# Output projection and SwiGLU by seven block products, tokens stationary, with two of four weight sums made by accumulating DMAs

## The chip, the cores and the metric

One core of a Trainium2 chip runs the whole program. The metric is the device time in microseconds (us) of one execution, as the median of several runs.

## What is computed

One encoder block over 512 tokens of 2048 features, everything in float32. Cut to what matters here:

```python
h = rms_norm(x, norm_mix)
z = h @ w_in                                   # q, k, v, u and two gates
merged = gate_a * (y_a @ w_branch_a) + gate_b * (y_b @ w_branch_b)
x = x + merged @ w_out                         # 2048 x 2048: the output projection
gu = rms_norm(x, norm_ffn) @ w_gate_up         # 2048 x 11264
x = x + (silu(gu[..., :5632]) * gu[..., 5632:]) @ w_down     # 5632 x 2048
return rms_norm(x, norm_final)
```

`y_a` is chunked attention and `y_b` a pooling mixer; the change leaves both as they are.

## The kernel before, in words

Activations lie with features on the partitions and the 512 tokens along the free axis. A float32 operand is split exactly into two float32r parts, `hi` and `lo = value - hi`, and each product is three matmuls into one PSUM group: lo x hi, hi x hi, hi x lo. In `product` (L183 to L186) the weights are the stationary operand (128x128) and the tokens move (128x512).

Weights come in units of four contraction tiles by 256 output columns (512 KB). For each unit SP issues one load (L123), ScalarE (ACT) makes `hi` (L132), VectorE (DVE) makes `lo` (L141). A unit's 24 matmuls follow in `panel` (L188), which then runs `step()`: one step of each side job in the list `active` (evacuations, norms, splits of activations), and then the `lo` of a unit three ahead. Each engine works through its own instructions in the order in which the code emits them, and so do the two DMA queues used, SP's and GpSimd's (POOL's).

The stages in order: q, k, v with attention beside them; u and the pooling mixer; gates and merge, where `evac_a` (L669) leaves a merged tile in `T` and `merged` (L674) splits it into `MH`, `ML`; the output projection (`evac_o`, L712, adds the residual, which comes back from `xt_dram`); SwiGLU in four blocks of hidden tiles, gate and up panels (`evac_g`, `evac_up`) and then the down panels, which add into `X1` in `evac_d` (L804). The last four hidden tiles are multiplied with tokens stationary (L859 to L863), so that the last sums, the final norm and the stores go token tile by token tile (`evac_y`, `store`).

## Time and profile before

| | us |
|---|---|
| median of 3 runs (2622.86 to 2624.26) | 2624.05 |
| span of the profiled execution, first to last instruction | 2621.3 |
| PE (TensorE) busy in it | 2608.7 |
| DVE busy | 1040.0 |
| ACT busy | 757.8 |

The profile gives only the span of its execution, not a time of its own; the median of the runs lies 2.75 us above it, which is taken as what lies around a span. A matmul's row lasts 0.39 us, since matmuls are pipelined; the distance between two starts is its cost. Idle time of DVE, ACT and POOL costs nothing by itself; PE's does.

### The profile page before, as it was taken

Reading aid. Unit: us, or ns where it says so; the run is one execution under the profiler, and the core shown is the slowest. Engines: PE = TensorE matmul, PEld = TensorE weight load, DVE = VectorE, ACT = ScalarE, POOL = GpSimd, SP = SyncE. Lnnn points to the kernel's source line nnn. Section 1 sums busy time; section 2 is a strip of 40 time slices with the busy share of each in tenths; the row PEclk is TensorE's granted clock in tenths of the full one; section 3 lists DMA queues with packets and bytes.
Section 4 is the critical chain, followed back from the end, with each engine's and each line's share of the span. In section 5 each row is a group of like instructions: output and inputs, shape, how many; then the busy total and the mean of one; then the engine's idle time right before and its main releaser. Section 6 shows DMA issues by size and latency. Waiting matters only on the chain.

```text
span 2621.3 us, 28748 instructions
## 1 busy us (share of the span) xinstructions
PE 2608.7 (100%) x11947; PEld 2158.0 (82%) x11947; DVE 1040.0 (40%) x1462; ACT 757.8 (29%) x1046; POOL 27.9 (1%) x75
## 2 busy tenths in 40 slices
PE   9999999999999999999999999999999999999998
PEld 7888888888888888888888888888888888888887
DVE  6455556433343334444333332333332333333353
ACT  5344433322232223232222212222212222222243
POOL 0000000000000000000000000000000000000003
PEclk9999999999999999999999999999999999999999
DMA  6422232233333333333333323333333332333242
GB/s 206 129 85 85 84 90 86 87 94 96 96 97 97 97 97 110 121 122 98 97 97 97 97 97 97 97 97 97 98 99 97 98 98 78 96 117 97 83 143 81
DMA packets 253474, 264.09 MB, mean 101 GB/s; under 512 B 9160, under 2 KB 241424, under 8 KB 253344
## 3 DMA queue, kind: packets, MB, share of 16 engines
q1 hardware_dynamic: 252032, 260.22, 31.7%
q8 instruction: 93, 1.52, 0.2%
q10 hardware_dynamic: 1152, 1.97, 0.2%
q14 instruction: 37, 0.30, 0.0%
q0 software_dynamic: 160, 0.07, 0.0%
HBM read 253.79 MB, written 8.43 MB: 100 GB/s over the span
## 4 chain that ended last, share of the span: by engine, by line
PE 99%; DMA 1%; ACT 0%; DVE 0%; issue 0%; SPq 0%; ACTq 0%; DVEq 0%
PE psd L184 30%; PE psd L186 30%; PE psd L185 30%; PE psd L430 1%; PE psd L432 1%; PE psd L431 1%; PE psa L477 1%; PE psa L557 1%; PE psa L523 1%; PE psa L476 1%; PE psa L186 0%; PE psa L184 0%; PE psa L185 0%; DMA wl<-in_w_down 0%; PE psa L323 0%; PE psa L799 0%
## 5 line engine op out<-in xcount | busy, mean ns | idle before, releaser
L141 DVE TENSOR_TENSOR lo<-raw,hi 128x1024 fp32r<-128x1024 f32 (+3 forms) x473 | 551.8, 1169 | 1142.3 <-ACT hi L132 1142.0
L132 ACT ACTIVATE hi<-raw 128x1024 fp32r<-128x1024 f32 (+3 forms) x473 | 477.7, 1012 | 1316.5 <-PE psd L186 1022.2
L185 PE MATMUL psd<-h2h,hi 128*128 128x512 f32 x1408 | 547.7, 389 | 0.0
L184 PE MATMUL psd<-h2h,lo 128*128 128x512 f32 x1408 | 547.7, 389 | 0.0
L186 PE MATMUL psd<-h2l,hi 128*128 128x512 f32 x1408 | 547.7, 389 | 0.0
L184 PE MATMUL psd<-xh,lo 128*128 128x512 f32 x864 | 341.4, 395 | 0.0
L185 PE MATMUL psd<-xh,hi 128*128 128x512 f32 x864 | 336.6, 390 | 0.0
L186 PE MATMUL psd<-xl,hi 128*128 128x512 f32 x864 | 336.6, 390 | 0.0
L185 PEld LDWEIGHTS psd<-h2h,hi 128*128 128x128 f32 x1408 | 264.3, 188 | 54.9
L186 PEld LDWEIGHTS psd<-h2l,hi 128*128 128x128 f32 x1408 | 264.3, 188 | 54.9
L184 PEld LDWEIGHTS psd<-h2h,lo 128*128 128x128 f32 x1408 | 264.3, 188 | 54.9
L184 PE MATMUL psd<-hidh,lo 128*128 128x512 f32 x640 | 250.5, 391 | 1.0 <-DVE xt L805 1.0
L186 PE MATMUL psd<-hidl,hi 128*128 128x512 f32 x640 | 249.1, 389 | 0.0
L185 PE MATMUL psd<-hidh,hi 128*128 128x512 f32 x640 | 249.0, 389 | 0.0
L184 PEld LDWEIGHTS psd<-xh,lo 128*128 128x128 f32 x864 | 162.2, 188 | 36.4 <-issue 2.4
L186 PEld LDWEIGHTS psd<-xl,hi 128*128 128x128 f32 x864 | 162.2, 188 | 34.2
L185 PEld LDWEIGHTS psd<-xh,hi 128*128 128x128 f32 x864 | 162.3, 188 | 32.0
L184 PEld LDWEIGHTS psd<-hidh,lo 128*128 128x128 f32 x640 | 120.1, 188 | 26.6 <-DVE xt L805 1.9
L186 PEld LDWEIGHTS psd<-hidl,hi 128*128 128x128 f32 x640 | 120.1, 188 | 25.1
L185 PEld LDWEIGHTS psd<-hidh,hi 128*128 128x128 f32 x640 | 120.2, 188 | 24.5
L185 PE MATMUL psd<-mh,hi 128*128 128x512 f32 x256 | 99.6, 389 | 0.0
L184 PE MATMUL psd<-mh,lo 128*128 128x512 f32 x256 | 99.6, 389 | 0.0
(197 smaller groups left out, 2345.1 us busy)
## 6 DMA issues: line engine op xcount, KB each, us to landing
raw<-in_w_gate_up SPq DMA_DIRECT2D x176, 512.0 KB, 3.5
raw<-in_w_in SPq DMA_DIRECT2D x127, 512.0 KB, 3.8
raw<-in_w_down SPq DMA_DIRECT2D x56, 512.0 KB, 3.5
raw<-in_w_out SPq DMA_DIRECT2D x32, 512.0 KB, 3.5
raw<-in_w_branch_b SPq DMA_DIRECT2D x16, 512.0 KB, 3.4
raw<-in_w_branch_a SPq DMA_DIRECT2D x16, 512.0 KB, 3.4
raw<-in_w_down SPq DMA_DIRECT2D x16, 384.0 KB, 3.3
xt_dram<-xt SPq DMA_DIRECT2D x16, 256.0 KB, 4.8
```

What stands on the lines that cost most here:

```text
L132: nc.scalar.activation(hi_t[i][:, :nk], raw_t[i][:, :nk], AF.Copy)
L141: nc.vector.tensor_tensor(lo_t[i][:, :nk], raw_t[i][:, :nk], hi_t[i][:, :nk].bitcast(F32), op=ALU.subtract)
L184: mm(ps, wl, ah, start=start, stop=False)
L185: mm(ps, wh, ah, start=False, stop=False)
L186: mm(ps, wh, al, start=False, stop=stop)
L430: mm(o, XH[kk][:, tok], hi[:, k], start=first, stop=False, skip_group_check=True)
L431: mm(o, XH[kk][:, tok], lo[:, k], start=False, stop=False, skip_group_check=True)
L432: mm(o, XL[kk][:, tok], hi[:, k], start=False, stop=final, skip_group_check=True)
L476: mm(o, q[:, tok], k[:, :n], start=True, stop=False)
L477: mm(o, q[hi_half, tok], kl[hi_half, :n], start=False, stop=True)
L523: nc.tensor.transpose(tp[b][:, o:o + P], sc[sb][:, sc0 + kt * P:sc0 + (kt + 1) * P], ident)
L557: mm(o_ps[:, kt * P:], VS[i, kt][:, hh * 2 * DH:(hh + 1) * 2 * DH], part[b][:, c:c + n], start=done == 0, stop=done == n_mm - 1)
```

## The change

The early stages, to the merge, stay as they are, apart from where tiles lie: the pool `slots` shrinks from 64 to 31 tiles, x^T has a pool of its own, x^T is no longer spilled to DRAM, and a merged tile goes from `evac_a` to `m_dram` by a POOL DMA in place of being split.

From the output projection on, three matrix products are cut into jobs. A job takes eight contraction tiles and 1024 output columns for all 512 tokens and is a 2x2 by 2x2 block product: the tokens fall into two halves, the contraction tiles into even and odd ones, the columns into two times 512. In place of eight block products it makes seven (Strassen's scheme in Winograd's form), `P1 P5 P6 P3 P7 P2 P4`, each in two units of 12 matmuls (two token tiles, two contraction tiles, three matmuls). Tokens are now stationary and weights move, 128x512. There are 36 jobs of 14 units and, at the end, two of 7 (half the contraction): four for `w_out`, 22 for `w_gate_up` (11 with the first half of the contraction, 11 with the second), 12 for `w_down`.

- **Token side**, `build_forms`: for each product a sum of token quarters is split into `hi` and `lo`, on ACT and DVE, as a generator that goes one product a `step()`. 19 halves are built.
- **Weight side**: of each unit pair the quarters 11, 22 and 21 are loaded. The sum 11+12 (tile `t1`) is a plain SP load of 11 and, behind it, a POOL DMA of 12 that accumulates into the same tile; 22+12 (`t3`) likewise. The other two sums, `t1`+22 and 21+(`t1`+22), are made by DVE in `t_to` (L851, L855). `hi2_to` (ACT, L863) and `lo2_to` (DVE, L871) split what a unit needs. The `t1` tiles have three buffers, and a `t1` is read until the sum for P4; the other quarters have six.
- **Outputs**: products accumulate in PSUM where the scheme allows it; what has to be combined is copied out by ACT after P1, P5, P6 (L906, L911, L916) and by DVE after P3, P7, P2 (L918, L923, L929); after P4 by DVE (L933) where an earlier partial result is added, else by ACT. Partial results and residuals are added by accumulating POOL DMAs into the tile (L908, L913, L920) or, in the `w_down` jobs but the last two, from the tile into DRAM (L1070); others are stored to DRAM by POOL DMAs (`x1p`, `x1d`, `gp`).
- **Turning**: since tokens come out on the partitions, `x1_ready` and `hidden` transpose on PE (`turned`, L960): 240 transposes of 128x128. The 64 transposes of the old end (L799) go.
- Between the merge and the first job `drain()` emits all steps of the first forms before the first unit's `hi` and `lo`.

The core of the diff:

```diff
-N_SLOTS = 64
+N_SLOTS = 31
...
+PRODUCTS = ("P1", "P5", "P6", "P3", "P7", "P2", "P4")
+NP = len(PRODUCTS)
+NPAIR = 4
+N_RAW2 = 6
+N_C = 6
+LOAD_AHEAD = 7
+T_BY_DMA = True
...
-        nc.vector.tensor_tensor(T[m], T[m], s, op=ALU.add)
...
-    def merged(ms):
-        for m in ms:
-            MH[m], ML[m] = split(T.pop(m), "m")
-            yield
...
+        nc.vector.tensor_tensor(s, T.pop(m), s, op=ALU.add)
+        m_dram[m] = tc.dram_tile([P, 512], F32, name=f"m_dram{m}")
+        nc.gpsimd.dma_start(m_dram[m], s)
...
+    def build_forms(forms, h, half):
+        a11, a12 = half[:, :, 0, 0:256], half[:, :, 1, 0:256]
+        a21, a22 = half[:, :, 0, 256:512], half[:, :, 1, 256:512]
...
+        tt = nc.vector.tensor_tensor
+        plan = [("P1", a11, 1, None), ("P5", s, 1, lambda: tt(s, a22, a21, op=ALU.subtract)),
+                ("P6", s, -1, lambda: tt(s, s, a11, op=ALU.add)),
+                ("P3", s, 1, lambda: tt(s, s, a12, op=ALU.subtract)),
+                ("P7", s3, 1, lambda: tt(s3, a11, a21, op=ALU.subtract)), ("P2", a12, 1, None), ("P4", a22, 1, None)]
+        for p, src, sign, make in plan:
+            if make:
+                make()
+            hi, lo = forms[p][:, prs, 0], forms[p][:, prs, 1]
+            nc.scalar.activation(hi, src, AF.Copy, scale=float(sign))
+            yield
+            if sign > 0:
+                tt(lo, src, hi.bitcast(F32), op=ALU.subtract)
+            else:
+                nc.vector.scalar_tensor_tensor(lo, src, -1.0, hi.bitcast(F32), op0=ALU.mult, op1=ALU.subtract)
+    def build_merged(forms, kb):
+        hs = []
+        for h in range(2):
+            half = yield from new_half()
+            for j in range(4):
+                nc.sync.dma_start(half[:, j // 2, j % 2], m_dram[8 * kb + 4 * h + j])
+            hs.append(half)
+            yield
+        for h in range(2):
+            yield from build(forms, h, hs[h])
+    for i in range(n_blk):
+        panel(KD, XH, XL, lambda oc, ps, i=i: evac_gate(2 * i + oc, ps))
+        if i == n_blk - 1:
+            XH = XL = None
+            xtiles.close()
...
+            active.append(build_merged(fo, 0))
+            spacing[0] = 0
+        panel(KA, YAH, YAL, lambda oc, ps, i=i: evac_a(2 * i + oc, ps))
+    drain()
+    midpool.close()
+    early.close()
...
+    class Job:
+        def quarter(self, s, f, h):
+            r0 = (self.k0 + 4 * h) * P
+            v = self.w[r0:r0 + 4 * P, self.c[f]:self.c[f] + 512]
+            return v.rearrange("(k s p) c -> s p k c", s=2, p=P)[s]
...
+    def plan_loads():
+        for j in jobs:
+            for h in range(j.nh):
+                loads.append((j.at("P1", h), j, "11", h))
+                loads.append((j.at("P5", h) - (4 if T_BY_DMA else 0), j, "t1" if T_BY_DMA else "12", h))
+                loads.append((j.at("P6", h), j, "22", h))
+                if T_BY_DMA:
+                    loads.append((j.at("P7", h) - 4, j, "t3", h))
+                loads.append((j.at("P2", h), j, "21", h))
...
+    def load2_to(n):
+        while loads and loads[0][0] <= n:
+            _, j, q, h = loads.pop(0)
+            t = rawtile(j, q, h)
+            s, f = {"11": (0, 0), "12": (0, 1), "21": (1, 0), "22": (1, 1), "t1": (0, 0), "t3": (1, 1)}[q]
+            nc.sync.dma_start(wide(t), j.quarter(s, f, h))
+            if q[0] == "t":
+                nc.gpsimd.dma_start(wide(t), j.quarter(0, 1, h), accum_op=ALU.add)
...
+        while st2["t"] < min(n, len(wunits)):
+            i = st2["t"]
+            j, p, h = wunits[i]
+            r = {q: t for (q, hh), t in j.raw.items() if hh == h}
+            run = r.get("t1", r.get("11"))
+            lo2_to(i - j.nh + 1)
...
+            elif p == "P6":
+                nc.vector.tensor_tensor(run, run, r["22"], op=ALU.add)
...
+            elif p == "P4":
+                nc.vector.tensor_tensor(r["21"], r["21"], run, op=ALU.add)
+            st2["t"] += 1
+    def hi2_to(n):
+        while st2["hi"] < min(n, len(wunits)):
+            i = st2["hi"]
+            t_to(i + 1)
+            hi_t[-1 - i] = staged("hi", f"w{i}")
+            nc.scalar.activation(hi_t[-1 - i], source(i), AF.Copy)
+    def lo2_to(n):
+        while st2["lo"] < min(n, len(wunits)):
+            i = st2["lo"]
+            hi2_to(i + 1)
+            lo_t[-1 - i] = staged("lo", f"w{i}")
+            nc.vector.tensor_tensor(lo_t[-1 - i], source(i), hi_t[-1 - i].bitcast(F32), op=ALU.subtract)
...
+        X = Y = Z = None
+        a = p5 = u2 = None
+        for n, p in enumerate(PRODUCTS):
...
+            for h in range(j.nh):
+                i = j.base + n * j.nh + h
+                load2_to(i + LOAD_AHEAD)
+                t_to(i + SPLIT + 1)
+                hi2_to(i + SPLIT)
+                hi, lo = wide(hi_t.pop(-1 - i)), wide(lo_t.pop(-1 - i))
+                for t in range(2):
+                    for k in range(2):
+                        fh, fl = forms[p][:, 2 * h + k, 0, TOK[t]], forms[p][:, 2 * h + k, 1, TOK[t]]
+                        last = h == j.nh - 1 and k == 1
+                        mm(ps[:, t], fh, lo[:, k], start=first, stop=False, skip_group_check=True)
+                        mm(ps[:, t], fh, hi[:, k], start=False, stop=False, skip_group_check=True)
+                        mm(ps[:, t], fl, hi[:, k], start=False, stop=last, skip_group_check=True)
+                if h == j.nh - 1:
+                    if p == "P1":
+                        a = ctile()
...
+                    elif p == "P5":
...
+                    elif p == "P6":
+                        u2 = ctile()
+                        nc.scalar.activation(u2, X, AF.Copy, scale=-1.0)
+                    elif p == "P3":
+                        nc.vector.tensor_tensor(u2, u2, Y, op=ALU.subtract)
+                        if j.acc:
+                            nc.gpsimd.dma_start(u2, j.acc["12"], accum_op=ALU.add)
+                        j.done("12", u2)
+                    elif p == "P7":
+                        nc.vector.tensor_tensor(p5, p5, X, op=ALU.subtract)
+                        j.done("22", p5)
+                        if j.acc:
+                            c21 = ctile()
+                            nc.sync.dma_start(c21, j.acc["21"])
+                    elif p == "P2":
+                        nc.vector.tensor_tensor(a, a, Z, op=ALU.add)
+                        j.done("11", a)
+                    elif p == "P4":
+                        if j.acc:
+                            nc.vector.tensor_tensor(c21, c21, X, op=ALU.add)
+                        else:
+                            c21 = ctile()
+                            nc.scalar.activation(c21, X, AF.Copy)
+                        j.done("21", c21)
+                step()
...
+    def turned(src, th, half, scale):
+        for c2 in range(2):
+            ps = bank2("a")
+            for c in range(2):
+                for t in range(2):
+                    nc.tensor.transpose(ps[:, (2 * c + t) * P:(2 * c + t + 1) * P],
+                                        src[:, t, (2 * c2 + c) * P:(2 * c2 + c + 1) * P], ident)
+            yield
...
+    def x1_ready(p, b, c):
+        th, fb = int(b[0]) - 1, int(b[1]) - 1
+        nc.gpsimd.dma_start(x1d[p, b], c)
+        yield
+        for t in range(2):
...
+            yield from build(gu_forms[p], fb, halves.pop((p, fb)))
...
+    def hidden(p, th, gate, up):
+        for t in range(2):
+            nc.scalar.activation(gate[:, t], gate[:, t], AF.Silu, scale=r2[:, 2 * th + t:2 * th + t + 1])
+        yield
+        for t in range(2):
+            nc.vector.scalar_tensor_tensor(up[:, t], up[:, t], r2[:, 2 * th + t:2 * th + t + 1], gate[:, t],
+                                           op0=ALU.mult, op1=ALU.mult)
+            yield
+        yield
+        if p not in hid:
+            hid[p] = yield from new_half()
+        yield from turned(up, th, hid[p], None)
+        if th == 1:
+            yield from build_down(p)
...
+                nc.gpsimd.dma_start(gp[p, b], c)
+                return
+            got[b] = c
+            if b == "11":
+                active.append(hidden(p, 0, got["11"], got["12"]))
+            elif b == "21":
+                active.append(hidden(p, 1, got["21"], got["22"]))
...
+    def d_done(b, p):
+        def done(blk, c):
+            if b < n_down - 1:
+                nc.gpsimd.dma_start(x1d[p, blk], c, accum_op=ALU.add)
+            else:
+                last_done(p, blk, c)
+        return done
...
+    order = [("o", kb, p) for kb in range(2) for p in range(2)] + [("g", 0, p) for p in range(NG)]
+    for p in range(NG):
+        order.append(("g", 1, p))
+        if p >= 2 and p % 2 == 0 and p < NG - 1:
+            order += [("d", p // 2 - 1, 0), ("d", p // 2 - 1, 1)]
+    order += [("d", b, p) for b in (n_down - 2, n_down - 1) for p in range(2)]
...
+    load2_to(LOAD_AHEAD - 2)
+    lo2_to(SPLIT - 1)
```

**DVE at the first job.** What stands there before the change, at the last merged tiles (`sg`, `ml`), and then the first `lo` of the output projection:

```order
L672 TENSOR_TENSOR sg_603_5724<-sg_603_5724,sg_689_7410 128x512
L213 TENSOR_TENSOR ml_699_7490<-sg_597_5532,mh_698_7489 128x512
L213 TENSOR_TENSOR ml_701_7496<-sg_602_5709,mh_700_7495 128x512
L213 TENSOR_TENSOR ml_703_7500<-sg_603_5724,mh_702_7499 128x512
L141 TENSOR_TENSOR lo163_7519<-raw163_7393,hi163_7505 128x1024
L141 TENSOR_TENSOR lo164_7549<-raw164_7434,hi164_7535 128x1024
```

The same place after it; `fP1` to `fP7` are the forms of the seven products, `s` and `s3` the running sums, `half` the token quarters, `low0` the `lo` of the job's first unit:

```order
L716 TENSOR_TENSOR s_644_7484<-half_642_7427 128x512
L727 TENSOR_TENSOR fP5_638_7390<-s_644_7484,fP5_638_7390 128x2x256
L717 TENSOR_TENSOR s_644_7484<-s_644_7484,half_642_7427 128x512
L729 SCALAR_TENSOR_TENSOR fP6_638_7391<-s_644_7484,fP6_638_7391 128x2x256
L718 TENSOR_TENSOR s_644_7484<-s_644_7484,half_642_7427 128x512
L727 TENSOR_TENSOR fP3_638_7392<-s_644_7484,fP3_638_7392 128x2x256
L719 TENSOR_TENSOR s3_644_7485<-half_642_7427 128x512
L727 TENSOR_TENSOR fP7_638_7393<-s3_644_7485,fP7_638_7393 128x2x256
L727 TENSOR_TENSOR fP2_638_7394<-half_642_7427,fP2_638_7394 128x2x256
L727 TENSOR_TENSOR fP4_638_7395<-half_642_7427,fP4_638_7395 128x2x256
L871 TENSOR_TENSOR low0_7608<-r11_647_7592,hiw0_7606 128x1024
L871 TENSOR_TENSOR low1_7612<-r11_648_7594,hiw1_7610 128x1024
```

In place of three splits of merged tiles, 20 instructions of the forms, of which the last 10 are shown, now stand between the last `evac_a` and `low0`.

**DVE in the SwiGLU stage.** Before, evacuations of gate panels (L758) between the `lo` of weight units:

```order
L141 TENSOR_TENSOR lo214_9291<-raw214_9203,hi214_9277 128x1024
L758 TENSOR_TENSOR sil_815_9295<-psd_813_9184,r2_8636 128x512
L758 TENSOR_TENSOR sil_816_9310<-psd_814_9185,r2_8636 128x512
L141 TENSOR_TENSOR lo215_9329<-raw215_9233,hi215_9315 128x1024
L141 TENSOR_TENSOR lo216_9359<-raw216_9263,hi216_9345 128x1024
```

After, in a job of the second half of `w_gate_up`: an L871 for each unit, sums (L855), the evacuations after P3, P7 and P2 (L918, L923, L929), and a step of the forms (L727):

```order
L871 TENSOR_TENSOR low288_13625<-rt3_1038_13406,hiw288_13609 128x1024
L918 TENSOR_TENSOR c_1051_13600<-c_1051_13600,psy_1046_13517 128x1024
L727 TENSOR_TENSOR fP4_1043_13488<-half_1005_12935,fP4_1043_13488 128x2x256
L871 TENSOR_TENSOR low289_13646<-rt3_1040_13429,hiw289_13629 128x1024
L871 TENSOR_TENSOR low290_13664<-r21_1047_13538,hiw290_13650 128x1024
L855 TENSOR_TENSOR r21_1047_13538<-r21_1047_13538,rt1_1031_13289 128x1024
L923 TENSOR_TENSOR c_1048_13554<-c_1048_13554,psx_1042_13467 128x1024
L871 TENSOR_TENSOR low291_13684<-r21_1049_13562,hiw291_13667 128x1024
L855 TENSOR_TENSOR r21_1049_13562<-r21_1049_13562,rt1_1033_13310 128x1024
L871 TENSOR_TENSOR low292_13702<-r21_1047_13538,hiw292_13688 128x1024
L929 TENSOR_TENSOR c_1045_13509<-c_1045_13509,psy_1056_13686 128x1024
L871 TENSOR_TENSOR low293_13726<-r21_1049_13562,hiw293_13709 128x1024
```

An evacuation, which waits for the last matmul of its product, now stands directly ahead of the `lo` of the unit after the next; in one of these three places a step of the forms stands between.

**POOL's queue there.** Before, POOL has nothing between the masks of the attention and the last token tiles. After, the DMAs of the second-half gate and up job 9; behind each row, in brackets, what it waits for (DMAHW are SP's loads, DMASW POOL's own DMAs):

```order
L908 DMA c_1288_17088<-gp9_11_7576 128x1024 [waits DMASW4_49,Activation_49]
L913 DMA c_1291_17133<-gp9_22_7579 128x1024 [waits DMASW5_49,Activation_49]
L830 DMA rt1_1293_17162<-in_w_gate_up 128x2x512 [waits DMAHW3_49,DMASW6_49]
L830 DMA rt1_1295_17185<-in_w_gate_up 128x2x512 [waits DMAHW4_49,DMASW7_49,DVE_49]
L920 DMA c_1294_17179<-gp9_12_7577 128x1024 [waits DMASW0_49]
L830 DMA rt3_1301_17285<-in_w_gate_up 128x2x512 [waits DMASW2_49,DMAHW1_49,DMASW1_49,Activation_49]
L830 DMA rt3_1303_17309<-in_w_gate_up 128x2x512 [waits DMAHW3_49,DMAHW5_49,DMAHW2_49,DVE_49]
```

L830 are the accumulating halves of the weight sums, for jobs ahead; L908, L913 and L920 add the first half's result into this job's outputs. L920, the addition after P3, stands behind the `rt1` DMA of the next job's second unit pair.

## Rows read from the trace of the kernel before

**Rows 1.** The page, parts 1 and 4: busy time; last chain by engine.

```profile
PE 2608.7 (100%) x11947; PEld 2158.0 (82%) x11947; DVE 1040.0 (40%) x1462; ACT 757.8 (29%) x1046; POOL 27.9 (1%) x75
...
PE 99%; DMA 1%; ACT 0%; DVE 0%; issue 0%; SPq 0%; ACTq 0%; DVEq 0%
```

**Rows 2.** Stages: busy us (x instructions) of each engine, granted clock, DMA share, GB/s.

```profile
992.30:1166.30 174.00, 174.00 (x769) 144.07 (x768) 69.28 (x78) 50.36 (x61) 0.00 (x0) 1.00 0.36 117
1166.30:2566.20 1399.90, 1398.91 (x6193) 1157.50 (x6192) 494.42 (x545) 345.69 (x402) 0.00 (x0) 1.00 0.32 99
```

**Rows 3.** Matmuls of the output projection in order of time: start, length, instruction.

```profile
1099.73 0.39 PE L186 MATMUL psd<-ml,hi 128*128 128x512 f32 x1
...
1103.81 0.39 PE L186 MATMUL psd<-ml,hi 128*128 128x512 f32 x1
```

**Rows 4.** Matmul groups of the changed stages by shape: count, busy us, mean ns.

```profile
L184 PE MATMUL psd<-h2h,lo 128*128 128x512 f32 x1408 | 547.7, 389 | 0.0
...
L184 PE MATMUL psd<-hidh,lo 128*128 128x512 f32 x640 | 250.5, 391 | 1.0 <-DVE xt L805 1.0
...
L184 PE MATMUL psd<-mh,lo 128*128 128x512 f32 x256 | 99.6, 389 | 0.0
```

**Rows 5.** One tile's instructions (`wl`, the last weights): shapes with counts.

```profile
L186 PE MATMUL psd<-wl,hidh x68: 279/389/398, 2567.6 to 2612.6; 128*128 128x512 f32 x60, 128*128 128x256 f32 x8
```

**Rows 6.** Transposes among matmuls, PE in order of time.

```profile
2515.96 0.60 PE L799 MATMUL psa<-ident,xt 128*128 128x128 f32 x4
...
2516.63 0.39 PE L185 MATMUL psd<-hidh,hi 128*128 128x512 f32 x1
```

**Rows 7.** Groups by shape, DVE and ACT: columns as in rows 4.

```profile
L141 DVE TENSOR_TENSOR lo<-raw,hi 128x1024 fp32r<-128x1024 f32 x423 | 517.4, 1225 | 1068.6 <-ACT hi L132 1068.3
...
L805 DVE TENSOR_TENSOR xt<-psd,xt 128x512 f32<-128x512 f32 x64 | 43.0, 688 | 44.7 <-PE psd L186 44.7
...
L213 DVE TENSOR_TENSOR hidl<-up,hidh 128x512 fp32r<-128x512 f32 x44 | 30.5, 692 | 30.8 <-ACT hidh L212 30.8
...
L759 ACT ACTIVATE sil<-sil 128x512 f32<-128x512 f32 x44 | 27.8, 632 | 97.1 <-DVE sil L758 97.1
...
L216 DVE SCALAR_TENSOR_TENSOR h2l<-xt,gains,h2h 128x512 fp32r<-128x512 f32 x16 | 12.0, 752 | 1.3 <-ACT h2h L215 1.3
```

**Rows 8.** PE's first matmuls after a wait, in order of time.

```profile
10.07 0.63 PE L185 MATMUL psa<-xh,hi 128*128 128x512 f32 x1
10.50 0.63 PE L186 MATMUL psa<-xl,hi 128*128 128x512 f32 x1
```

**Rows 9.** Chain of waits in order of time: start, length, instruction.

```profile
2513.12 0.61 DVE xt L805
2513.78 0.50 PE psd L184
```

**Rows 10.** The end, in order of time.

```profile
2612.59 0.28 PE L186 MATMUL psd<-wl,hidh 128*128 128x256 f32 x1
2612.91 0.42 DVE L832 TENSOR_TENSOR y<-psd,y 128x256 f32<-128x256 f32 x1 [1.01 <-PE psd L186]
```

**Rows 11.** DMA at its fullest and in the SwiGLU stage, columns as in rows 2.

```profile
10.00:15.00 5.00, 5.00 (x22) 4.03 (x21) 2.07 (x3) 2.96 (x6) 0.00 (x0) 1.00 1.06 383
1400.00:1460.00 60.00, 60.00 (x267) 49.67 (x266) 20.31 (x21) 15.13 (x17) 0.00 (x0) 1.00 0.31 98
```

**Rows 12.** DMA issues: count, KB each, median us to landing.

```profile
raw<-in_w_gate_up SPq DMA_DIRECT2D x176, 512.0 KB, 3.5
...
grow<-in_norm_mix SPq DMA_DIRECT2D x1, 8.0 KB, 1.5
...
grow<-in_norm_ffn POOLq DMA_DIRECT2D x1, 8.0 KB, 3.3
```

**Rows 13.** POOL's issues of DMAs of 16 and 8 rows, in order of time.

```profile
2.15 0.49 POOL L301 DMA_DIRECT2D grow<-in_norm_ffn  x1
2.64 0.51 POOL L302 DMA_DIRECT2D grow<-in_pool_scale  x1
```

More of the change, by code (lines that the diff above doesn't have):

```diff
@@ L75, in hybrid_block_kernel @@
     KF = F // P
-    assert S == 512 and DH == 64 and sum(FF_BLOCKS) == KF
+    assert S == 512 and DH == 64
     x = x[0]
@@ L695, in hybrid_block_kernel, with forms_pool, new_forms @@
         step()
+    late = ctx.enter_context(ExitStack())
+    pools = {}
+    righted = ctx.enter_context(ExitStack())
+    def forms_pool(which, side):
+        pools[which] = (righted if side == "right" else late).enter_context(
+            tc.tile_pool(name=f"forms{which}", bufs=1, side=side, reuse_waits="tile"))
+    def new_forms(which):
+        serial[0] += 1
+        return {p: pools[which].tile([P, NPAIR, 2, 256], F32R, tag=f"f{p}", name=f"f{p}_{serial[0]}") for p in PRODUCTS}
+    live = [0]
@@ L867 @@
+    while active or later:
+        step()
 _INS = ["x", "norm_mix", "w_in", "rel_bias", "pool_w", "pool_scale", "w_branch_a", "w_branch_b",
```

471 lines of the change are left out of this document (269 added, 202 removed).

## The prediction, made before the changed kernel ran

> **What bounds the kernel now.** The page first: TensorE (PE) is busy for the whole span, and 99% of the chain that ended last is PE; DVE is at 40%, ACT at 29% [rows 1]. The table by stages says the same of the part that the change touches: in the output projection PE is busy 174.00 of 174.00 us, in the SwiGLU stage 1398.9 of 1399.9, at a granted clock of 1.00, while DVE does 0.35 to 0.40 us a us and the DMA engines are a third busy [rows 2]. So before, only PE's work counts. What a matmul costs is its distance to the next: 18 matmuls of the output projection start 4.08 us apart, 0.2267 us each [rows 3].
>
> **What goes: matmuls.** The three products have 3 x 256, 3 x 1408 and 3 x 640 matmuls of 128x512 [rows 4], and 3 x 60 more plus 3 x 8 of half width with the last weights [rows 5], in all 7104 full ones. Seven block products in place of eight leave 36 jobs x 168 + 2 x 84 = 6216, of the same shape and with as many stationary loads. 888 x 0.2267 = **-201.3 us**. The part before the output projection keeps its 992.3 us [rows 2].
>
> **What comes on PE.** 240 transposes for 64, 176 more. Four of them and the matmul behind them take 0.67 us [rows 6], so 0.11 each: **+19.4 us**.
>
> **The start of the first job.** Before, PE went on without a gap into the output projection [rows 2]. After, the forms of the first job stand ahead of its first `lo` on DVE. After the last matmul of the gates come two additions on DVE, 2 x 0.69; then seven forms with a running sum, each a chain DVE 0.69, ACT 0.63, DVE 0.69; six instructions of 0.69 that need no chain; and the `lo` of 1.23 [rows 7]: 1.4 + 14.1 + 4.1 + 1.2 = 21, with the hand-overs 22 us. The first weight loads land within that (the old tiles are free once POOL has written the last merged tile: about 5 us, and 3.5 us of load [rows 12]). Then PE starts from idle. At the kernel's start, after a wait, matmuls go 0.43 us apart [rows 8], twice the later distance, which is the pace of the lower of PE's two levels (1.2 and 2.4 GHz); I take 2 us for that. **+24 us**, with ends 16 (ACT and DVE overlap better) and 30.
>
> **DVE in the jobs.** A unit is 12 x 0.2267 = 2.72 us of PE. Per job DVE has 14 splits and 4 sums at 1.23, three or four evacuations of twice 0.69, taken as 1.23, and in places 11 instructions of a form or four of `hidden` (0.69 to 0.75 [rows 7]): 26 to 37 us of the job's 38. On average it fits (about 80%). It doesn't fit where the order puts an evacuation, which waits for the last matmul of unit i, directly ahead of the `lo` of unit i+2. A DVE evacuation starts 0.32 us after the start of the last matmul [rows 10], a half-wide one, so 0.20 after PE could have gone on. PE starts 0.66 us after the start of a 0.69 us DVE instruction that it waits for [rows 9]. So `lo` is there 0.20 + 1.23 + 1.20 = 2.63 us after unit i ends, and unit i+1 covers 2.72: a clean evacuation costs nothing, with 0.1 to spare. A form or `hidden` step in between does. By the order, of 131 evacuations 17 have one such instruction behind them, 19 two, 11 one of 0.75, and 2 a longer row: 17 x 0.6 + 19 x 1.3 + 11 x 0.65 + 2 x 4.5 = **+50 us**; ends 20 and 80, as the margin of 0.1 turns out.
>
> **POOL's queue in `w_gate_up`'s second half (11 jobs).** DVE's `hidden` instruction for the first token half waits for L920, due in unit 13. L920 stands behind the `rt1` DMA of the next job's second pair, that behind its plain load, and this SP load waits for a `t1` tile that is free only after DVE's L855, about 9.4 units into the job. Load 3.5 us [rows 12], a POOL issue of 0.5 [rows 13] to perhaps 1, then L920: a POOL DMA lands 1.8 us later than the like from SP [rows 12], so 5.3 us. That is unit 12.9 to 13.4, and DVE, stopped there, holds the next `lo`. Between 0 and 3.5 us a job I take 1.5: **+17 us**. The Trainium skill (DMA: Bandwidth & Descriptors, Anatomy of one DMA) gives about 2 us plus bytes over 436 GB/s for a POOL DMA, 3.2 us for 512 KB; by that estimate this term would be near 0 and the sum 17 us lower. The trace has no POOL DMA of that size.
>
> **The DMA engines.** The jobs move 518 quarters of 0.524 MB (148 of them accumulating), 68 partial results or residuals in (51 accumulating), 40 accumulated into DRAM and 60 out: 360 MB, of which 125 MB accumulate. Filled, with the 2 KB rows that the jobs use too, the engines moved 383 GB/s at a share of 1.06, 361 at 1.00 (1 KB rows: 98 at 0.31, 316) [rows 11]. At the price of a plain transfer 360 MB take 996 us of the roughly 1480 that PE needs. What an accumulating transfer costs no row shows. Its ends are one pass over the engines, like a load, and three, a load, a read back and a store: 347 us for each further pass. I take the middle, two passes, 1343 us, 91% of PE's time; loads then land later, and the loads of a job's first quarters are issued behind the late `t1` load, with some 4.6 us of slack. About 0.8 us a job: **+30 us**, ends 0 and what the first rival says. The Trainium skill (DMA: Bandwidth & Descriptors, Rules for kernel authors) says that an accumulating DMA reads its destination and writes it later; that makes two reads to a write, by which estimate the sum stands as it is. No row of this trace bears on it.
>
> **The end.** From the last matmul's 2612.59 + 0.12 to 2621.3 are 8.6 us [rows 10]. After, a last tile twice as wide goes through DVE, ACT and POOL in turn: **+3 us**.
>
> **Sum**, against the profiled span of 2621.3: -201.3 + 19.4 + 24 + 50 + 17 + 30 + 3 gives 2563.4; with the 2.75 us that the median lies above the span, **2566 us**, 2.2% faster.
>
> **Rivals.**
> *The DMA engines become the bound (slower).* At three passes the jobs need 996 + 694 = 1690 us of DMA; 992.3 + 24 + 1690 + 11.6 + 2.75 = 2721 us. It decides from 2.7 passes on, where DMA time reaches the 1593 us that are left of the old span. For: the share rises from a third to over 0.9 at two passes already. Against: PE's own needs leave room up to 2.2 passes. 26%.
> *All waits are covered* (DVE gets ahead between evacuations, loads are early): without the 50, 17 and 30 it is 2469 us. For: DVE and DMA averages below 1. Against: the order, which puts the evacuation ahead of the `lo`. Anything under 2500: 16%.
> *POOL's issue becomes the bound.* 300 DMAs in 1480 us are one per 4.9 us; 16 rows take 0.49 us to issue [rows 13], and these have 128 or 256. If issue went by rows, 8 us each, 2400 us for the jobs and 3400 in all. Against: 8 rows take as long, 0.51 us [rows 13], so most of it is a fixed part. 3%.
>
> **How the numbers follow.** 2500 to 2619: 50%; below: 16%; within 0.2% of 2624 (2619 to 2629), where stalls eat just the gain: 5%; above, the two slower cases: 29%. A measurement of this kernel tells about 0.2% from no change. Faster 0.66, same 0.05, slower 0.29. The range leaves out the lowest 8% and the highest 12%: 2485 to 2715. The forecast's own range is 2500 to 2619.
>
> **What would show it.** Right: PE's matmuls 0.227 us apart within units; one gap of some 24 us near 990 us; short PE waits for DVE's L871 right after L918, L923, L929, L933 where L727 or L1027 lies between; DMA share of 0.8 to 0.95. Wrong: a DMA share of 1.0 in the jobs with PE waiting for loads (first rival), PE waits for L863 or L871 that wait for DMAs in most jobs (my 30 us are too few), or hardly any waits of PE.

## The result, and the profile after

| | before | after |
|---|---|---|
| median of the runs, us | 2624.04 | 2720.73 (2719.74 to 2721.38) |
| ratio, 95% interval | | 1.0369 (1.0355 to 1.0384) |
| span of the profiled execution, us | 2621.3 | 2718.0 |

The change makes the kernel 3.7% slower. The forecast was 2566 us, 2.2% faster, in a range of 2485 to 2715: the sign is wrong, and the range misses the time by 6 us. One rival's figure, 2721 us for three passes over the DMA engines, is nearly the measured time. That turns out to be a coincidence of two numbers, as the experiments show.

Parts 1 to 4 of the page of the changed kernel, beside [rows 1]: busy time, the granted clock and the DMA share in 40 slices, the last chain by engine.

```profile
PE 2526.9 (93%) x11221; PEld 2029.2 (75%) x11221; DVE 1566.0 (58%) x1848; ACT 1161.4 (43%) x1499; POOL 336.3 (12%) x390
...
PEclk9999999999999998989999999899999999899997
DMA  5322222233233348986877888767959779779595
...
PE 42%; DMA 10%; DVE 5%; issue 3%; ACT 2%; POOL 0%; ACTq 0%; DVEq 0%; POOLq 0%; SPq 0%
```

PE is no longer alone on the chain: it holds 42% of the span there, DMA 10% and DVE 5%, and the clock falls now and then.

Stages of the changed kernel, beside [rows 2], in the same columns: the part ahead of the first job, the gap, all jobs, the end.

```profile
0.00:1008.60 1008.60, 1005.24 (x4765) 817.86 (x4765) 447.05 (x769) 331.20 (x517) 15.33 (x73) 1.00 0.32 101
1008.60:1029.50 20.90, 0.04 (x2) 0.01 (x1) 15.70 (x24) 9.89 (x16) 5.46 (x5) 0.55 1.04 282
1029.50:2697.00 1667.50, 1521.58 (x6456) 1211.37 (x6456) 1094.92 (x1034) 810.19 (x949) 308.81 (x307) 0.96 0.80 214
2697.00:2718.00 21.00, 0.00 (x0) 0.00 (x0) 8.31 (x23) 10.13 (x19) 6.68 (x6) 0.58 0.54 200
```

The DMA share over the jobs is 0.80, not 1, yet the jobs take 1667.5 us, where 6216 matmuls at 0.2267 make 1409. The first part has the same matmuls as before but takes 1008.6 us, not 992.3.

Three jobs of `w_gate_up` in the same columns: one of the first half of the contraction, most of the first job of the second half, and the second job of the second half.

```profile
1425.60:1465.00 39.40, 39.40 (x170) 31.67 (x169) 25.09 (x21) 18.52 (x18) 5.36 (x7) 1.00 0.80 236
1661.80:1697.00 35.20, 35.20 (x157) 28.92 (x155) 22.68 (x19) 18.71 (x19) 6.91 (x7) 1.00 0.93 276
1708.20:1762.00 53.80, 44.24 (x184) 34.62 (x184) 35.57 (x38) 25.51 (x32) 7.49 (x7) 0.91 0.69 175
```

The first two run without a gap, at shares of 0.80 and 0.93. The third stands idle 9.6 us, at a share of only 0.69. All eleven jobs of the second half end in a gap of 6.6 to 8.7 us. What ends it is in the chain of waits around the third job's end (start, length, what):

```profile
1741.09 1.24 DVE r L855
...
1742.38 3.83 DMA rt<-in_w_gate_up
...
1746.90 0.44 POOL rt L830
...
1747.64 12.33 DMA c<-gp
...
1760.06 0.06 DVE c L1027
...
1760.73 1.23 DVE low L871
...
1762.01 0.80 PE psx L900
1762.80 0.43 PE psx L901
```

This is the prediction's path, step by step: L855 frees the `t1` tile, the plain load lands 3.8 us later, POOL issues its accumulating DMA and then L920 (`c<-gp`), DVE stops at L1027 until L920 lands, and the next job's first `lo` (L871) stands behind L1027. The landing takes 12.3 us, where 5.3 stood in the sum. PE starts again with matmuls 0.43 us apart, as in [rows 8].

Waits of that kernel: DVE's for L920, PE's for `lo` (two kinds of PSUM tile), SP's for the tile that L855 frees (us in total, times, longest):

```profile
DVE c L1027 <- DMA c<-gp: 93.3, 11, 9.9
...
PE psx L900 <- DVE low L871: 124.0, 36, 20.9
PE psy L900 <- DVE low L871: 17.3, 17, 1.6
...
SPq L828 <- DVE r L855: 969.1, 36, 32.9
```

The DMAs land later throughout than in [rows 12] (3.5 us for a load): DMA issues of the changed kernel, median us to landing last.

```profile
r<-in_w_gate_up SPq DMA_DIRECT2D x132, 512.0 KB, 7.5
...
rt<-in_w_gate_up POOLq DMA_DIRECT2D x88, 512.0 KB, 9.0
...
c<-gp POOLq DMA_DIRECT2D x33, 512.0 KB, 11.8
```

A second loss has nothing to do with waits. Matmuls 1 and 19 of a gapless stretch in the job at 1425.6, then in the job at 1661.8 (start, length, instruction), beside [rows 3]:

```profile
1429.80 0.39 PE L900 MATMUL psx<-low,fP 128*128 128x512 f32 x1
...
1434.02 0.39 PE L900 MATMUL psy<-low,fP 128*128 128x512 f32 x1
...
1669.73 0.39 PE L902 MATMUL psy<-hiw,fP 128*128 128x512 f32 x1
...
1673.81 0.39 PE L902 MATMUL psx<-hiw,fP 128*128 128x512 f32 x1
```

Eighteen matmuls take 4.22 us in the one and 4.08 us in the other, both at a granted clock of 1.00. The jobs with the slower pace (0.2344 in this stretch) are the 23 that read their token forms from the pool `formsA`; jobs on `formsB` go at 0.2267.

### The profile page after: what moved, and what is told of

Same layout as the page of the kernel before. It is cut to its first block, busy times and chain, and to the rows that moved or that the text cites. A ratio compares the mean times of both kernels' runs of the same rounds, so it can differ in the third digit from the quotient of the medians.

```text
span 2718.0 us, 29427 instructions
## 1 busy us (share of the span) xinstructions
PE 2526.9 (93%) x11221; PEld 2029.2 (75%) x11221; DVE 1566.0 (58%) x1848; ACT 1161.4 (43%) x1499; POOL 336.3 (12%) x390
## 4 chain that ended last, share of the span: by engine, by line
PE 42%; DMA 10%; DVE 5%; issue 3%; ACT 2%; POOL 0%; ACTq 0%; DVEq 0%; POOLq 0%; SPq 0%
PE psx L900 8%; PE psx L901 8%; PE psx L902 8%; PE psy L900 6%; PE psy L901 6%; PE psy L902 6%; DMA c<-gp 6%; DVE low L871 3%; PE psa L960 1%; DMA rt<-in_w_down 1%; DMA rt<-in_w_gate_up 1%; DMA c<-x1p 1%; ACT hiw L863 1%; DMA rt<-in_w_out 1%; DVE r L855 1%
## 5 line engine op out<-in xcount | busy, mean ns | idle before, releaser
L900 PE MATMUL psx<-low,fP 128*128 128x512 f32 x1184 | 488.7, 413 | 139.3 <-DVE low L871 124.0
L901 PE MATMUL psx<-hiw,fP 128*128 128x512 f32 x1184 | 478.2, 404 | 0.0
L902 PE MATMUL psx<-hiw,fP 128*128 128x512 f32 x1184 | 477.2, 403 | 0.0
L863 ACT ACTIVATE hiw<-r 128x1024 fp32r<-128x1024 f32 x296 | 311.8, 1057 | 284.6 <-PE psx L902 150.2
L871 DVE TENSOR_TENSOR low<-r,hiw 128x1024 fp32r<-128x1024 f32 x296 | 361.1, 1226 | 124.6 <-ACT hiw L863 124.3
L900 PE MATMUL psy<-low,fP 128*128 128x512 f32 x888 | 355.2, 400 | 17.6 <-DVE low L871 17.3
L871 DVE TENSOR_TENSOR low<-rt,hiw 128x1024 fp32r<-128x1024 f32 x222 | 271.6, 1224 | 172.6 <-ACT hiw L863 172.3
L901 PE MATMUL psy<-hiw,fP 128*128 128x512 f32 x888 | 350.5, 395 | 0.0
L902 PE MATMUL psy<-hiw,fP 128*128 128x512 f32 x888 | 350.3, 394 | 0.0
L863 ACT ACTIVATE hiw<-rt 128x1024 fp32r<-128x1024 f32 x222 | 234.3, 1055 | 107.4 <-PE psy L902 26.4
L902 PEld LDWEIGHTS psx<-hiw,fP 128*128 128x128 f32 x1184 | 229.8, 194 | 55.0
L901 PEld LDWEIGHTS psx<-hiw,fP 128*128 128x128 f32 x1184 | 231.2, 195 | 49.5
L900 PEld LDWEIGHTS psy<-low,fP 128*128 128x128 f32 x888 | 167.6, 189 | 63.3 <-DVE low L871 23.3
L902 PEld LDWEIGHTS psy<-hiw,fP 128*128 128x128 f32 x888 | 167.5, 189 | 39.1
L901 PEld LDWEIGHTS psy<-hiw,fP 128*128 128x128 f32 x888 | 167.6, 189 | 36.3
L830 POOL DMA_DIRECT2D rt<-in_w_gate_up x88 | 106.7, 1212 | 699.4 <-DMA rt<-in_w_gate_up 513.9
## 6 DMA issues: line engine op xcount, KB each, us to landing
x1d<-c POOLq DMA_DIRECT2D x48, 512.0 KB, 13.2
```

What stands on the lines that cost most here:

```text
L830: nc.gpsimd.dma_start(wide(t), j.quarter(0, 1, h), accum_op=ALU.add)
L863: nc.scalar.activation(hi_t[-1 - i], source(i), AF.Copy)
L871: nc.vector.tensor_tensor(lo_t[-1 - i], source(i), hi_t[-1 - i].bitcast(F32), op=ALU.subtract)
L900: mm(ps[:, t], fh, lo[:, k], start=first, stop=False, skip_group_check=True)
L901: mm(ps[:, t], fh, hi[:, k], start=False, stop=False, skip_group_check=True)
L902: mm(ps[:, t], fl, hi[:, k], start=False, stop=last, skip_group_check=True)
```

## Experiments

Theory A: the order of POOL's queue delays L920, DVE stops in order, PE runs out of `lo`, and its clock falls. Theory B: the DMA engines bound the jobs (the first rival). Theory M: the slower pace hangs on where the two operands lie in the on-chip memory. Times are medians; the kernel before stood at 2623.6 to 2623.9 beside them.

| run | us | ratio to before, 95% | L1027 waits for L920, us |
|---|---|---|---|
| changed kernel | 2720.73 | 1.0369 (1.0355 to 1.0384) | 93.3 |
| e3_lead | 2594.66 | 0.9893 (0.9879 to 0.9908) | none listed |
| e9_lead2 | 2598.75 | 0.9911 (0.9896 to 0.9926) | 13.2 |
| e1_late | 2619.02 | 0.9981 (0.9971 to 0.9990) | none listed |
| e10_t3dve | 2708.82 | 1.0322 (1.0305 to 1.0340) | 94.7 |
| e4_dve | 2598.15 | 0.9900 (0.9885 to 0.9915) | none listed |
| e2_pad | 2704.63 | 1.0306 (1.0289 to 1.0324) | |
| e5_pad96 | 2688.25 | 1.0243 (1.0226 to 1.0260) | |
| e12_before_pad | 2618.70 | 0.9982 (0.9973 to 0.9991) | |
| e6_lead_pads | 2554.57 | 0.9736 (0.9722 to 0.9751) | |
| e7_dve_pads | 2556.11 | 0.9742 (0.9727 to 0.9756) | |
| e11_mixed | 2552.53 | 0.9729 (0.9715 to 0.9744) | |
| e8_x1 | 2558.59 | 0.9753 (0.9738 to 0.9767) | |

### The order of the queue

**e3_lead** moves L920 ahead of the next job's weight sums in POOL's queue:

```diff
-                loads.append((j.at("P5", h) - (4 if T_BY_DMA else 0), j, "t1" ...
+                loads.append((j.at("P5", h) - (1 if T_BY_DMA else 0), j, "t1" ...
```

> Edit: the t1 loads of a job are planned one unit ahead of P5 in place of four, so that SP issues them and POOL their accumulating DMAs three units later, behind L920. Theory A: L920 no longer waits in POOL's queue for the t1 load, lands some 8 us earlier, and the gaps at the ends of the second-half w_gate_up jobs go: 2580 to 2640, unless t1 now comes too late for the ACT instruction that splits it (13 us from issue to use against 16 us of the two landings under load), which would cost up to 3 us a job in 36 jobs, 2640 to 2720. Theory B (DMA engines bound): within 15 us of 2721.

It took 126 us off. POOL in order of time in the second job of the second half, 26 us into it (the changed kernel issues L920 39 us into it):

```profile
1710.12 0.86 POOL L920 DMA_DIRECT2D c<-gp  x1 [11.13 <-DVE c L918]
1710.79 1.42 POOL L830 DMA_DIRECT2D rt<-in_w_gate_up  x1
```

Stages of the same run: the first and second job of the second half, then all jobs.

```profile
1645.90:1684.00 38.10, 38.10 (x169) 31.28 (x168) 24.62 (x21) 20.90 (x21) 6.82 (x7) 1.00 1.00 282
1684.00:1728.50 44.50, 41.52 (x186) 32.76 (x185) 35.41 (x37) 25.52 (x32) 8.61 (x8) 1.00 0.90 227
...
1028.80:2578.00 1549.20, 1494.11 (x6456) 1190.81 (x6456) 1093.92 (x1034) 808.86 (x948) 307.73 (x307) 0.99 0.87 231
```

The first row speaks against theory B most plainly: a whole job with the DMA share at 1.00 and PE busy for all of it. The same bytes now take 1549 us of jobs in place of 1667. The third job's 53.8 us are 44.5, and the clock stays at 1.00.

**e9_lead2** asks which weight sum in front of L920 does the harm: with 2 in place of 4, the first `t1` sum stays ahead of L920, and only the second, whose tile L855 frees, goes behind it.

```diff
-                loads.append((j.at("P5", h) - (4 if T_BY_DMA else 0), j, "t1" ...
+                loads.append((j.at("P5", h) - (2 if T_BY_DMA else 0), j, "t1" ...
```

> Edit on the changed kernel: the t1 loads planned two units ahead of P5 in place of four. POOL then issues the next job's first t1 sum ahead of L920 and the second behind it; the first one's tile is free long before, the second one's only after L855. If what delays L920 is the load that waits for its tile (SP stopped behind L855): the gaps go as in e3_lead, 2590 to 2615. If any weight sum ahead of L920 in POOL's queue delays it so: half the gain or less, 2655 to 2721.

Nearly all of the gain is there. So POOL's order is harmful where a DMA waits in it for a load that waits for a tile; a sum whose load is early does little.

**e1_late** leaves every queue as it is and lets DVE come to L1027 later:

```diff
-                active.append(hidden(p, 0, got["11"], got["12"]))
+                active.append(wait_then(4, hidden(p, 0, got["11"], got["12"])))
...
-                active.append(hidden(p, 1, got["21"], got["22"]))
+                active.append(wait_then(2, hidden(p, 1, got["21"], got["22"])))
```

> Edit: hidden for the first token half of a w_gate_up job starts four steps later and for the second half two steps later; every DMA, every matmul and every tile stays. Theory A (DVE, in order, stops at L1027 for the accumulating DMA L920, PE then runs out of lo tiles at the next job's start, and the clock falls behind the gap): the 11 gaps of 7 to 8.7 us at the ends of the second-half jobs go, and the slow matmuls behind them, 11 x 10 to 14 us; time 2570 to 2625. Theory B (the DMA engines bound the jobs, as in the first rival): the bytes are the same, so the time stays within 15 us of 2721. Theory C (DVE has no room, the wait only moves to the next instruction): 2665 to 2700.

102 us less with the same DMAs in the same order: what L920's lateness costs is DVE standing still in front of the next `lo`. PE's waits of this run:

```profile
PE psx L900 <- DVE low L871: 45.1, 46, 20.9
...
PE psa L960 <- DMA c<-x1p: 5.8, 2, 3.9
```

The 20.9 is the gap ahead of the first job, which all these runs share. That e3_lead gains 24 us more lies mostly in the same queue a stage earlier: in the last `w_out` jobs, too, the DMA into the tile that PE turns (`c<-x1p`, again L920) stands behind weight sums. That wait is listed here and is gone in e3_lead. The last `w_out` job and the first of `w_gate_up` together, in the stages' columns, in e1_late and then in e3_lead:

```profile
1153.60:1267.70 114.10, 96.30 (x401) 74.57 (x400) 77.58 (x84) 70.29 (x124) 18.76 (x22) 0.91 0.70 195
```

```profile
1152.90:1250.80 97.90, 89.55 (x402) 69.93 (x400) 77.25 (x84) 66.61 (x115) 19.76 (x23) 0.98 0.83 235
```

That is 16 us, of a difference of 18.6 between the two spans (2617.6 and 2599.0).

### The load on the DMA engines

**e10_t3dve** takes half of the accumulating weight DMAs away and leaves L920 where it is: `t3` becomes a plain load, and DVE adds.

```diff
-                    loads.append((j.at("P7", h) - 4, j, "t3", h))
+                    loads.append((j.at("P7", h) - 4, j, "12", h))
...
-        q = {... "P7": "t3" if T_BY_DMA else "12", ...
+        q = {... "P7": "12", ...
...
-            elif p == "P7" and not T_BY_DMA:
+            elif p == "P7":
                 nc.vector.tensor_tensor(r["12"], r["12"], r["22"], op=ALU.add)
```

> Edit on the changed kernel: the sum t3 is made by DVE from a plain load, t1 stays an accumulating DMA with its place in both queues. L920 stands behind the late t1 as before, with 74 accumulating DMAs of 512 KB fewer around it. If the queue's order sets the gaps: L920 is issued as late as before and lands 12 us after issue or a few us less; 2680 to 2725. If the load on the DMA engines sets them: the gaps shrink by half or more, 2660 or less.

It took 12 us off. In the third job's place the DMA share is 0.61, and DVE's waits for L920 stay as they were:

```profile
DVE c L1027 <- DMA c<-gp: 94.7, 11, 10.2
```

So halving these DMAs does not bring the gaps down. From the start of the first second-half job to the end of the last, where all eleven gaps lie, e10_t3dve is only some 3 us shorter.

**e4_dve** takes away all 148, and with them 74 plain loads, since 11 and 22 are then loaded once instead of twice (the expectation below counts the 148 as becoming plain loads; the edit leaves four loads of seven DMAs):

```diff
-T_BY_DMA = True
+T_BY_DMA = False
```

> Edit: the two sums of weight quarters that accumulating DMAs make are made by DVE from plain loads; 148 accumulating DMAs of 512 KB become plain loads, and DVE gets 148 more instructions of 1.23 us (4.9 us a job). Theory A: POOL's queue holds no weight sums any more, L920 goes out at once, and the gaps at the ends of the second-half jobs go; DVE, at some 26 to 37 us of a 38 us job before, is short in the jobs that build forms: 2620 to 2690. Theory B (the DMA engines bound the jobs): their share falls from 0.8 to about 0.65 and the time to 2600 or less. Theory C (DVE is the bound): slower than 2721.

The time, 2598 us, lies below theory A's range and inside theory B's, so by itself it speaks for B; the comparison with e3_lead speaks against it. DVE gets 169 us more work, and the jobs are no longer than in e3_lead. The DMA queues (packets, MB, share of 16 engines) of e3_lead in the first fence and of e4_dve in the second, and e4_dve's jobs in the stages' columns in the third:

```profile
q1 hardware_dynamic: 197888, 302.56, 34.2%
q0 software_dynamic: 64352, 162.10, 31.0%
```

```profile
q1 hardware_dynamic: 177760, 263.76, 30.2%
q0 software_dynamic: 24096, 84.49, 13.9%
```

```profile
1029.70:2575.30 1545.60, 1494.11 (x6456) 1190.49 (x6456) 1262.46 (x1181) 812.24 (x948) 128.54 (x163) 0.99 0.53 157
```

The difference of POOL's queue (q0) prices the accumulating DMA: 31.0% of 2599.0 less 13.9% of 2596.8 is 445 us for 77.6 MB, 174 GB/s. [Rows 11] have 361 GB/s at a share of 1 for plain transfers. So an accumulating DMA costs 2.1 passes over the engines. Three passes, on which the first rival's 2721 us rested, are excluded. The jobs' length in all is the same at a DMA share of 0.87 and of 0.53. That could be two effects that cancel, but it holds for single jobs too: the sixth of the first half in e3_lead, at a share of 0.84, and in e4_dve, at 0.43.

```profile
1409.80:1449.20 39.40, 39.40 (x170) 31.64 (x169) 25.11 (x21) 18.51 (x18) 7.14 (x8) 1.00 0.84 242
```

```profile
1412.20:1451.50 39.30, 39.30 (x169) 31.60 (x168) 29.61 (x26) 18.51 (x18) 2.14 (x4) 1.00 0.43 154
```

So theory B falls with its mechanism.

### The pace

The allocator gives these starts of the tiles in a partition, modulo 128 bytes, with the median distance of matmuls in gapless stretches:

| kernel | stationary | moving | us a matmul |
|---|---|---|---|
| before, x^T panels | weights 96 | 96 | 0.2267 |
| before, y_a and y_b panels | weights 96 | 32 | 0.2335 |
| after, x^T panels | weights 0 | 96 | 0.2333 |
| after, jobs on forms A | forms 96 | weights 0 | 0.2342 |
| after, jobs on forms B | forms 0 | weights 0 | 0.2267 |
| e2_pad, x^T panels | weights 32 | 96 | 0.229 |
| e2_pad, jobs on forms A | forms 96 | weights 32 | 0.2333 |
| e2_pad, jobs on forms B | forms 32 | weights 32 | 0.2267 |
| e5_pad96, x^T panels; jobs on A | 0 | 0 | 0.2267 |
| e5_pad96, y panels | weights 0 | 96 | 0.2333 |
| e6_lead_pads, all | 0 | 0 | 0.2267 |
| e12_before_pad, y panels | weights 96 | 96 | 0.2267 |

**e2_pad** came first, when only the place modulo 64 was suspected:

```diff
+    const.tile([P, 8], F32, name="pad")
     stage = ctx.enter_context(tc.tile_pool(name="stage", bufs=1))
```

> Edit: 32 unused bytes a partition ahead of the pool stage, nothing else. It moves stage, forms B and the pools slots and mid by 32 bytes; forms A and x^T lie from the top and stay. In the changed kernel jobs on forms A run at 0.234 us a matmul and jobs on forms B at 0.2267; A lies at 32 modulo 64 bytes, B and the staged weights at 0. Theory M (the pace depends on whether stationary and moving operand lie at the same place modulo 64): all jobs at 0.2267, 23 jobs x 14 units x 0.09 = 29 us less, the panels on x^T at 0.2267 in place of 0.234, some 13 us less, the panels on y_a and y_b stay slow; 2670 to 2690. Theory U (it is the side, or the traffic, not the place modulo 64): 2718 to 2724. Theory W (any operand at 32 modulo 64 is slow): forms B jobs become slow too, 15 jobs x 1.27 = 19 us more, 2740.

None of the three: the first part fell to 993.5 us, the jobs on A hardly changed. With these rows the table fits modulo 128, not 64.

**e5_pad96**, 96 bytes at the top, in front of x^T's pool:

```diff
+    ctx.enter_context(tc.tile_pool(name="padr", bufs=1, side="right")).tile([P, 24], F32, name="padr")
     xhl = xtiles.enter_context(
```

> Edit on the changed kernel: 96 unused bytes a partition at the top of the on-chip memory, so that forms A and x^T lie 96 bytes lower; stage, forms B, slots and mid stay. In the run with 32 bytes ahead of stage the panels on x^T became faster (the first part by 15 us), the jobs on forms A hardly (0.2342 to 0.2333 us a matmul). Before, after and that run together fit this: 0.2267 where the two operands of a matmul start at the same place modulo 128 bytes, up to 0.235 where not. Here forms A, x^T, staged weights and forms B all start at 0 modulo 128 (at 128 modulo 256 too, but not all at the same place modulo 512). Theory M128: jobs on forms A at 0.2267, 23 x 14 x 0.09 = 29 us less, and the first part 13 to 16 us less: 2670 to 2682. If a larger modulus counts: between 2690 and 2721. If the upper end of the memory is slow as such: the jobs on A stay at 0.234, 2703 to 2721.

The pace is as theory M has it. Matmuls 1 and 19 in a job on forms A:

```profile
1529.84 0.39 PE L903 MATMUL psy<-hiw,fP 128*128 128x512 f32 x1
...
1533.92 0.39 PE L903 MATMUL psx<-hiw,fP 128*128 128x512 f32 x1
```

4.08 us (the pad's line shifts the line numbers by one), and the first part ends at 993.8. The total fell by 32 us, less than the 39 to 51 expected: jobs on forms A without a wait are 1.2 us shorter each, as worked out, but the first `w_gate_up` job is 1.7 us longer and the last `w_down` job but one 2.9 us, so that in this kernel part of what PE gains is waited away.

**e12_before_pad** carries the finding to the kernel before: 64 bytes in front of the pool of y_a and y_b.

```diff
+            midpool.enter_context(tc.tile_pool(name="pad", bufs=1)).tile([P, 16], F32, name="pad")
             mid = midpool.enter_context(tc.tile_pool(name="mid", bufs=N_SLOTS_B, reuse_waits="tile"))
```

> Edit on the kernel before: 64 unused bytes a partition ahead of the pool mid, which holds the split y_a and y_b; nothing else moves. Before, the weights' hi and lo start at 96 modulo 128, mid at 32, and the panels on y_a and y_b go at 0.2335 us a matmul, all others at 0.2267. If the pace hangs on the operands' places modulo 128: the 768 matmuls of these panels go at 0.2267, 5 us less, 2618 to 2620. If these panels are slower for another reason: 2622 to 2625.

4.9 us where 5 were worked out, from 768 matmuls.

### Together, and what is left

**e6_lead_pads** is e3_lead with 864 bytes at the top and 544 in front of `slots`; **e7_dve_pads** has the same pads and all sums on DVE, as e4_dve; **e11_mixed** is e6_lead_pads with the edit of e10_t3dve.

```diff
+    const1.tile([P, 136], F32, name="pad1")
     slots = early.enter_context(...
...
+    ctx.enter_context(tc.tile_pool(name="padr", bufs=1, side="right")).tile([P, 216], F32, name="padr")
     xhl = xtiles.enter_context(...
```

> Edit: the t1 loads one unit ahead of P5 (as in e3_lead) and pads, 864 bytes at the top and 544 ahead of slots, so that forms A, forms B, x^T, y_a, y_b and the staged weights start at the same place modulo 2048. If the pace hangs on the place: 2594.7 - 29 (jobs on A) - 16 to 20 (first part) = 2545 to 2552, below both kernels. If it hangs on the upper end of the memory: the first part alone, 2575 to 2582.

> Edit: the same pads, and all four sums of weight quarters on DVE (as in e4_dve): the seven products without accumulating weight DMAs. Theory A (the DMA engines have room, DVE's order sets the waits): 2598 - 45 = 2553, within 8 us of e6_lead_pads, though it moves 77 MB less by accumulation. Theory B (DMA load costs time): more than 10 us below e6_lead_pads.

> Edit on e6_lead_pads: t3 by DVE, t1 by accumulating DMA. e6_lead_pads and e7_dve_pads stand within 2 us of one another, so one sum more or less on DVE should change nothing: 2548 to 2560. If DVE and the DMA engines were both near their limits, the even split would gain more: below 2545.

All three beat the kernel before by 2.6 to 2.7% and the changed kernel by 6%, though e6_lead_pads is 3 us above the 2545 to 2552 expected. Their intervals overlap: on balance, the two sums made by accumulating DMAs neither win nor lose time once L920 is out of their way. In single jobs they do: in the last `w_down` job but one PE still waits 10.5 us in one piece in e6_lead_pads, for an evacuation that waits for the residual's DMA, and 1.3 us in e7_dve_pads, whose last job is 6 us longer; the other jobs differ by 2 us or less either way. Against the kernel before with a pad of its own (e12_before_pad, 2618.7 us) the gain is 2.4 to 2.5%. That the 888 matmuls fewer bring it is argued, not shown: no run has eight products in the new form. The fastest median is e11_mixed, 2552.5 us, within the intervals of the other two.

**e8_x1** was to remove the waits of the last `w_out` jobs' transposes in e6_lead_pads.

```diff
-            active.append(wait_then(4 if b == "12" else 2, x1_ready(p, b, c)))
+            active.append(wait_then(6 if b == "12" else 4, x1_ready(p, b, c)))
```

> Edit on e6_lead_pads: x1_ready in the last output projection jobs starts two steps later (6 and 4 in place of 4 and 2), so that the transposes L960, which PE takes in order, stand further behind the accumulating DMA that fills their tile. In e3_lead the first three units of the jobs o(1,1) and g(0,0) are some 6 us longer each than units without a wait. If that is the wait for the tile: 5 to 12 us below e6_lead_pads. If the forms then come too late for g(0,0): up to 10 us above it.

Nothing was gained: 2558.6 us against 2554.6, with intervals that overlap. PE's waits, of e6_lead_pads and then of e8_x1, show that the tile was not what the transposes wait for, even ahead of the edit:

```profile
PE psa L962 <- ACT half L971: 4.9, 2, 3.1
```

```profile
PE psa L962 <- ACT half L971: 4.8, 2, 2.9
```

It is the copy of the transposes before out of PSUM, by ACT, with two banks in turn (L971 is L969 of the changed kernel).

## Why the prediction was wrong, by its own steps

Against the span of 2718.0 the sum gave 2563.4, 154.6 us too little. By the stages and runs above:

- **POOL's queue, +17.** This step failed, and the sign with it. Its path is the one in the chain, link by link, but its size is wrong. In the eleven jobs it is worth 100 us, the difference of the spans of the changed kernel and e1_late (102 by the medians). Another 16 us of the same queue lie in the last `w_out` job and the first of `w_gate_up`, where the sum has no such term; e3_lead, without either, has a span 119 us shorter. Three things were off. L920 landed 12.3 us after its issue where 5.3 stood in the sum: 3.5 for a load by SP at a DMA share of a third, and 1.8 by which a POOL DMA of 8 KB landed later than one from SP [rows 12]. The loads that SP holds back behind L855 go out in one burst just ahead of L920, which POOL issues at 1747.64; and in the gap at the job's end the DMA share is 1.09, in a job whose mean is 0.69. SP's issues, and then that gap in the stages' columns (granted clock third from the end):

```profile
1742.38 0.37 SPq L828 DMA_DIRECT2D rt<-in_w_gate_up  x1
1742.85 0.93 SPq L828 DMA_DIRECT2D r<-in_w_gate_up  x2
1743.83 0.46 SPq L927 DMA_DIRECT2D c<-gp  x1
...
1744.88 0.42 SPq L828 DMA_DIRECT2D rt<-in_w_gate_up  x1
```

```profile
1755.00:1762.00 7.00, 0.00 (x0) 0.00 (x0) 1.94 (x3) 0.00 (x0) 1.20 (x1) 0.73 1.09 267
```

  And the wait costs more than itself, since the clock falls: the gap of the job before and the 5.3 us after it hold 15 matmuls. The 13 of the second stretch would take 2.9 us at 0.2267.

```profile
1700.00:1708.20 8.20, 0.10 (x2) 0.01 (x1) 1.95 (x3) 0.00 (x0) 1.19 (x1) 0.72 1.09 267
1708.20:1713.50 5.30, 5.30 (x13) 4.14 (x14) 5.27 (x6) 2.28 (x3) 1.20 (x1) 0.50 0.95 201
```

  The Trainium skill (DMA: Bandwidth & Descriptors, Anatomy of one DMA) gives 2 us and bytes over 436 GB/s, an estimate of 3.2 us for these 512 KB; on loaded engines the trace has 12.3, and no run here shows one alone.
- **Matmuls, -201.3.** The count, 6216, is right; the pace of 0.2267 was carried over from [rows 3] to places where it doesn't hold: 23 jobs x 168 x 0.0076 = 29 us. The first part, held at 992.3, is 16.3 us longer, and goes back to 993.5 or 993.8 with a pad. A pool that moves was costed at nothing.
- **The end, +3.** From the start of the last matmul at 2696.5 to 2718.0 are 21.5 us, 12.8 more than before rather than 3. The sum had one last tile there; in the trace the outputs of all four token tiles are scaled and stored behind the last matmul, eight pieces one after the other on ACT alone (L1108, 2704.1 to 2712.9).
- **The start, +24.** A gap of 20.9 and a first unit 2.4 slower: 23.3. The work, two-engine chain included, was counted right.
- **Evacuations +50, DMA load +30, transposes +19.4.** In e3_lead the jobs stand 140 us above their matmuls' 1409. Less the 29 for pace that is 111; these terms, with the old transposes and gaps (10) and the cold first unit (2), made 111 too. Their split is less sure: PE's listed waits for L871 in the jobs add up to 33 us in e3_lead, a single one for DVE's L923, which waits for an `x1d` DMA, to 12.1. Transposes cost what was worked out: four take 0.44 us in the changed kernel's chain. What lies in shorter gaps was not told apart.
- **The rivals.** The first has the right time for a wrong reason: two passes, as the sum took them, are what was measured (2.1), the share was 0.80. The Trainium skill (DMA: Bandwidth & Descriptors, Rules for kernel authors) says that such a DMA reads its destination and writes it later; the measured 174 GB/s against 361 agree. The second rival, all waits covered, did not come either: with L920's wait and the slower pace both gone, e6_lead_pads stands at 2554.6 us, not 2469. POOL's issue, the third, takes 0.8 to 1.7 us a DMA, where 8 would have bound the jobs; POOL is busy for 12% of the span.

Added up: 119 - 17, 29, 16.3, 9.8 and -0.7 are 156.4 us, where 154.6 were to be found. That it closes to 2 us is partly luck: the profiled run of e3_lead was the slowest of its four, and by the medians the first term is 126 rather than 119. The text held what was needed for the sign: it put the DMA share at 0.91 and landings "later", but sized the one wait that decides by landings read at a third of that share. With 12.3 us in place of 5.3, L920 is 7 us later in 11 jobs; 77 us more make an estimate of 2643, above the kernel before.

## What to carry to other kernels

Where an in-order engine waits for a DMA, follow that DMA's queue back to a load that waits for a tile, and price its landing at the DMA load that the change makes, not at that of the trace before; then add what the clock takes after the gap. An issue moved by three units was worth 126 us here and cost nothing. And check at which place modulo 256 bytes the two operands of the matmuls start, since a pad of some bytes a partition was worth 3% of the matmul time here where they differed (0.234 against 0.2267 us).
